# Low parts of weights moved from ScalarE and a DMA to VectorE, and a part of the last norm moved forward

## The chip, the cores and the metric

The kernel runs on one core of a Trainium2 chip. What counts is the time of one execution on the device in microseconds; the smaller, the better. The executions of the kernel before took 827.84, 830.14 and 832.91 us, a median of 830.14.

## What is computed

One encoder block on 512 tokens with 1024 channels, in float32. Cut to what matters here:

```python
h = rms_norm(x, norm1_pre)
q, k, v, z, xbc, dt_raw, gates = split_cols(h @ w_in, IN_SPLITS)
attn_out = gqa_attention(rope(norm(q)), rope(norm(k)), v) @ w_attn_proj
ssd_out = ssd_branch(z, xbc, dt_raw, ...) @ w_ssd_proj
g_attn, g_ssd = split(sigmoid(gates), 2)
x = x + rms_norm((g_attn * attn_out + g_ssd * ssd_out) @ w_out, norm1_post)
gate, up = split(rms_norm(x, norm2_pre) @ w_gate_up, 2)
x = x + rms_norm((silu(gate) * up) @ w_down, norm2_post)
```

## The kernel before

**Products in three matmuls.** Each float32 operand is split into a high part, rounded to float32r, and a low part, the difference to the original. `mm3` (L177) makes a product of two such pairs: low by high (L178), high by low (L179), high by high (L180).

**The stream of weights.** `weights()` (L103) lists the weights in the order in which they are used, each with the way in which its low part is made. `presplit()` (L136) takes the next raw weight, which SP has loaded (three buffers), and lets ScalarE write the high part (L144). For "v" VectorE and for "g" GpSimd subtracts it from the raw weight (L149). For "d" ScalarE writes the negated high part (L146: the negative of the rounded value, as its output is float32r) and a DMA started by GpSimd adds the weight to it from memory (L147). High and low parts have four buffers each, so a new weight's parts wait until TensorE has used the fourth before.

**The order of the work.** The setup norms x, transposes h and makes q. Then `kvproj` (L397) multiplies by w_kv in three chunks of the eight blocks of 128 channels (0 to 2, 3 to 5, 6 and 7): for each block k four token tiles with three matmuls each. VectorE makes h at L294 and the low part of its transposed form hT at L184 for the same product. Twelve weights w_xbc follow, then attention. `weave` sets matmuls of z (`zproj`, two column halves n with four weights each) and of the first two gates between the steps of attention (scores L635 and L636, maxima L638 and exponentials L641 of the softmax, its transposes L653), then the other fourteen gates between those of the SSD. Attention needs VectorE for the maxima, the division and copies. A scheduler orders the instructions of VectorE, ScalarE and GpSimd; each engine runs its own queue in order.

**The end.** `down` (L1153) makes the last product of the FFN with seven products of quarter matrices in place of eight, in this order of PSUM targets: u, v, a, x, u, a, y. Each runs in four groups; for a group ScalarE and VectorE split weights (L1195, L1196) and activations (L1201, L1202), and GpSimd starts a DMA (L1225) that adds a second block of the weight to the first. `add` (L1245) sums the results in tiles c[t, n], where t is the token tile and n the column half. `begin(t)` loads the residual x2, takes the square sum of one half on ScalarE (L155) and multiplies that half by the gain (L1257); `finish(t)` does so for the other half (L1264), forms the reciprocal root and writes the sum with the residual out (L1270). For tiles 0 and 1 `between` calls them after blocks 4 to 7 of the last product y; for tiles 2 and 3 `begin` is called behind the fifth product and `finish` when y is done.

Of the kernel before, what the change touches and what calls it, by code (L numbers as in the profile page):

```python
# [14 lines left out]
ALU = mybir.AluOpType  # L15
# [45 lines left out]
class Block:  # L61
# [41 lines left out]
    def weights(self):  # L103

        a = self.a
        for k0, kn in ((0, 3), (3, 3), (6, 2)):
            yield a["w_kv"][:, k0 : k0 + kn, :], kn * 288, "v" if k0 == 0 else "d"
        for j in range(12):
            yield a["w_xbc"][j], 1024, "g" if j < 3 else "d"
        for n in range(2):  # L110
            for i in range(4):
                yield a["w_z"][n, i], 1024, "gd"[n]
        for j in range(2 * KD):
            yield a["w_g"][j], 1024, "d"
        for j in range(KD):
            yield a["w_ap"][j], 512, "g"
        for j in range(KD):
            yield a["w_sp"][j], 1024, "g"
        for j in range(KD):
            yield a["w_o"][j], 1024, "gggggvvv"[j]  # L120
# [1032 lines left out]
    def down(self, pool):  # L1153


        V, A, G, T = self.V, self.A, self.G, self.T
# [5 lines left out]
        r1 = [new("r1", [256], PAIRS) for _ in range(PAIRS)]  # L1162
# [3 lines left out]
        def blk(g, k, n):  # L1166

            j = n0 + k * PAIRS + 2 * g
            return wd[j : j + 2, :, n * 512 : n * 512 + 512].rearrange("k p c -> p k c")
# [3 lines left out]
        for k in range(1, n0):  # L1173
# [5 lines left out]
            if k == 1:  # L1179
                gain = [new("gn", [512], 2) for _ in range(2)]  # L1180
# [7 lines left out]
        c = {(t, 1): cs.pop() for t in (2, 3, 0, 1)}  # L1188
# [22 lines left out]
        a11, a12 = (lambda k: act[n0 + k][:, lo]), (lambda k: act[n0 + PAIRS + k][:, lo])  # L1211
# [4 lines left out]
        def product(dst, b, a, start, after=None, sums=None, by_token=None, then=None):  # L1216

            kept = []

            def prep(g):  # L1220
                w = wsplit(b(g))
                for i in range(2):
                    kept.append((asplit(a(2 * g + i)), [y[:, i * 512 : i * 512 + 512] for y in w]))
                if after:
                    G.dma_start(chain[g], after(g), accum_op=ALU.add)  # L1225

            def work(g):
                for k in (2 * g, 2 * g + 1):
                    x, wi = kept[k]
                    for t in range(1 if by_token else 2):  # L1230
                        mm3(dst[t], [y[:, t * P : t * P + P] for y in x], wi, start and k == 0)
                    if sums:
                        sums(k)
                if g == NG2 - 1:
                    if by_token:
                        by_token()
                        for x, wi in kept:
                            mm3(dst[1], [y[:, P : 2 * P] for y in x], wi)
                    if then:
                        then()  # L1240

            stages.extend((lambda g=g: prep(g), lambda g=g: work(g)) for g in range(NG2))

        def add(t, n, p, op=ALU.add):
            V.tensor_tensor(c[t, n], c[t, n], p, op)  # L1245

        half = {}

        def begin(t):

            x = [new("x2", [512], 4) if t < 2 else self.slot("a", [512], name="x2") for _ in range(2)]
            for i in range(2):
                self.load(x[i], self.x2_d[t][:, i * 512 : i * 512 + 512])
            ss = self.tiny(2, "ss")
            self.square_sum(ss[:, 0:1], c[t, 1], self.rstd[:, t : t + 1])
            V.tensor_scalar(ss[:, 0:1], ss[:, 0:1], 1.0 / D, EPS, ALU.mult, ALU.add)
            V.tensor_tensor(c[t, 1], c[t, 1], gain[1], ALU.mult)  # L1257
            half[t] = x, ss

        def finish(t):  # L1260
            x, ss = half[t]
            r2 = self.rstd[:, t : t + 1]
            self.square_sum(ss[:, 1:2], c[t, 0], r2)
            V.tensor_tensor(c[t, 0], c[t, 0], gain[0], ALU.mult)  # L1264
            v = self.tiny(1, "rv")
            V.tensor_scalar(v, ss[:, 1:2], 1.0 / D, ss[:, 0:1], ALU.mult, ALU.add)
            r = self.rsqrt(v, 1, True)
            V.tensor_tensor(r, r, r2, ALU.mult)
            for i in (1, 0):
                V.scalar_tensor_tensor(c[t, i], c[t, i], r, x[i], ALU.mult, ALU.add)  # L1270
                self.load(self.out[t * P : t * P + P, i * 512 : i * 512 + 512], c[t, i])

        u = [self.ps("sa") for _ in range(2)]
        a = [self.ps("mm") for _ in range(2)]
        x = [self.ps("sb") for _ in range(2)]
        v, y = [bank[t, 0] for t in (0, 1)], [bank[t, 0] for t in (2, 3)]
# [12 lines left out]
        def second(p):  # L1289
            for t in range(2):  # L1290
                add(2 + t, 1, p[t], ALU.subtract)

        def sums6():
            for t in range(2):
                c[2 + t, 0] = cs.pop()
                A.copy(c[2 + t, 0], u[t])
                add(2 + t, 1, u[t], ALU.subtract)
                add(t, 1, u[t], ALU.subtract)
                add(2 + t, 0, x[t])
                begin(2 + t)  # L1300

        def sums3():
            for t in range(2):
# [1 line left out]

        def last(t):
            add(t, 0, y[t - 2])
            finish(t)

        between = {4: lambda: begin(0), 5: lambda: begin(1), 6: lambda: finish(0), 7: lambda: finish(1)}  # L1310
        product(u, lambda g: chain[g], a11, True, lambda g: blk(g, 0, 1),
                lambda k: V.tensor_tensor(r1[k], a22(k), a21(k), ALU.subtract), then=third_weights)
        product(v, lambda g: raw(g, 1, 0), a12, False, None, lambda k: V.tensor_tensor(a21(k), a11(k), a21(k), ALU.subtract),
                then=sums2)
        product(a, lambda g: chain[g], lambda k: r1[k], True, lambda g: blk(g, 1, 1),
                lambda k: V.scalar_tensor_tensor(r1[k], r1[k], -1.0, a11(k), ALU.mult, ALU.subtract), then=lambda: second(a))
        product(x, lambda g: p3[g], a21, True, None,
                lambda k: V.scalar_tensor_tensor(a12(k), r1[k], -1.0, a12(k), ALU.mult, ALU.subtract), then=lambda: second(x))
        product(u, lambda g: chain[g], lambda k: r1[k], False, lambda g: blk(g, 1, 0), then=sums6)
        product(a, lambda g: raw(g, 1, 1), a12, False, then=sums3)  # L1320
        product(y, lambda g: chain[g], a22, False, None, lambda k: between.get(k, int)(), lambda: last(2))
        stages[0][0]()
        for i, (_, work) in enumerate(stages):
            if i + 1 < len(stages):
                stages[i + 1][0]()
            work()
        last(3)

    @staticmethod
# [121 lines left out]
```

## Time and profile before

| what | value |
|---|---|
| median of the three executions | 830.14 us |
| the profiled execution, its own time | 830.12 us |
| its span in the profile | 828.2 us |
| TensorE busy | 804.9 us, 97% |
| VectorE busy | 578.4 us, 70% |
| ScalarE busy | 465.8 us, 56% |
| GpSimd busy | 200.0 us, 24% |

The profile shows one execution. Busy shares are means over stages with different limits; what a stage waits for is read from its own stretch of the trace.

### The profile page before, as it was taken

How to read it: one execution, taken by the hardware profiler on the slowest of the kernel's cores; microseconds unless marked ns; L12 is line 12 of the kernel's file. 1: busy time of each engine (PE TensorE's matmuls, PEld its weight loads, DVE VectorE, ACT ScalarE, POOL GpSimd, SP SyncE). 2: the span in 40 equal slices, each digit the busy share in tenths (PEclk: the TensorE clock that was granted, in tenths of full speed). 3: DMA queues.
4: the chain of work that ended last, by engine and by line, in shares of the span. 5: the costliest groups of instructions: out<-in, count | busy, mean ns of one | idle time of the engine just before them, and what ended most of it. 6: DMA issues, size and time to landing. Idle time of an engine off the chain costs nothing.

```text
span 828.2 us, 12209 instructions
## 1 busy us (share of the span) xinstructions
PE 804.9 (97%) x4522; PEld 676.8 (82%) x4522; DVE 578.4 (70%) x999; ACT 465.8 (56%) x841; POOL 200.0 (24%) x162
## 2 busy tenths in 40 slices
PE   8899999999899999999999999999999999999994
PEld 7688887666676777777888798999999999888883
DVE  3959785656335456685783799788888878837988
ACT  7767875745844442166333656555555555536673
POOL 3443430100132244539451002000000100041200
PEclk9999999999999999999999999999999999999998
DMA  9757830620875665137335453667766664899642
GB/s 314 218 134 159 200 93 27 140 64 1 216 176 130 158 150 124 52 114 252 116 129 185 164 153 91 188 193 188 193 177 185 182 178 140 286 288 245 104 93 102
DMA packets 49658, 130.52 MB, mean 158 GB/s; under 512 B 5568, under 2 KB 5952, under 8 KB 49600
## 3 DMA queue, kind: packets, MB, share of 16 engines
q1 hardware_dynamic: 38048, 95.46, 33.7%
q0 software_dynamic: 11552, 34.30, 24.0%
q8 instruction: 35, 0.57, 0.3%
q14 instruction: 23, 0.19, 0.1%
HBM read 121.35 MB, written 8.39 MB: 157 GB/s over the span
## 4 chain that ended last, share of the span: by engine, by line
PE 83%; DVE 5%; DMA 4%; ACT 3%; issue 2%; POOL 1%; SPq 1%; DVEq 0%; ACTq 0%; POOLq 0%
PE sa L972 10%; PE mm L178 8%; PE mm L179 8%; PE mm L180 8%; PE sc L972 7%; PE sb L1125 4%; PE sa L1125 4%; PE mm L972 3%; PE sb L972 3%; PE mm L1125 3%; PE sc L178 3%; PE sc L180 3%; PE sc L179 3%; PE sc L677 2%; PE sa L179 2%
## 5 line engine op out<-in xcount | busy, mean ns | idle before, releaser
L144 ACT CAST whi<-raw 128x1024 fp32r<-128x1024 f32 (+3 forms) x69 | 68.0, 992 | 20.6 <-PE sc L180 9.8
L178 PE MATMUL mm<-hT,wlo 128*128 128x512 f32 x176 | 73.8, 419 | 2.1 <-DMA wlo<-in_w_g 2.1
L149 POOL TENSOR_TENSOR wlo<-raw,whi 128x1024 fp32r<-128x1024 f32 (+1 forms) x28 | 58.2, 2081 | 65.5 <-ACT whi L144 63.9
L180 PE MATMUL mm<-hT,whi 128*128 128x512 f32 x176 | 69.7, 396 | 0.0
L179 PE MATMUL mm<-hT,whi 128*128 128x512 f32 x176 | 69.3, 394 | 0.0
L1023 POOL DMA_DIRECT2D raw<-in_w_gu x19 | 16.4, 861 | 211.5 <-ACT x L1114 54.8
L1028 ACT CAST whi<-raw 128x512 fp32r<-128x512 f32 (+1 forms) x57 | 41.6, 762 | 33.9 <-DMA raw<-in_w_gu 12.9
L1029 DVE TENSOR_TENSOR wlo<-raw,whi 128x512 fp32r<-128x512 f32 (+1 forms) x57 | 47.8, 866 | 16.3 <-ACT whi L1028 16.3
L972 PE MATMUL sa<-R,whi 128*128 128x256 f32 x304 | 56.4, 283 | 0.0
L972 PEld LDWEIGHTS sa<-R,whi 128*128 128x128 f32 x304 | 47.5, 192 | 0.0
L146 ACT ACTIVATE wlo<-raw 128x1024 fp32r<-128x1024 f32 (+2 forms) x31 | 32.3, 1043 | 26.4 <-PE mm L178 24.4
L972 PE MATMUL sa<-R,wlo 128*128 128x256 f32 x152 | 43.1, 283 | 0.0
L178 PEld LDWEIGHTS mm<-hT,wlo 128*128 128x128 f32 x176 | 33.3, 189 | 11.8 <-issue 3.2
L147 POOL DMA_DIRECT2D wlo<-in_w_g x16 | 13.8, 863 | 112.6 <-ACT wlo L146 66.7
L179 PEld LDWEIGHTS mm<-hT,whi 128*128 128x128 f32 x176 | 33.3, 189 | 8.7 <-issue 2.4
L180 PEld LDWEIGHTS mm<-hT,whi 128*128 128x128 f32 x176 | 33.3, 189 | 7.6 <-issue 0.5
L638 DVE TENSOR_REDUCE nmax<-sa 128x1 f32<-128x512 f32 x32 | 21.6, 686 | 19.9 <-PE sa L636 19.7
L972 PE MATMUL sa<-h2T,b 128*128 128x256 f32 x228 | 30.5, 283 | 0.0
L641 ACT ACTIVATE pr<-sa,nmax 128x512 f32<-128x512 f32 x32 | 22.0, 688 | 14.6 <-DVE rc L643 7.4
L972 PEld LDWEIGHTS sa<-R,wlo 128*128 128x128 f32 x152 | 29.2, 192 | 0.0
L155 ACT ACTIVATE junk<-z 128x512 bf16<-128x512 f32 x8 | 5.0, 628 | 42.6 <-DVE z L785 42.5
L972 PEld LDWEIGHTS sa<-h2T,b 128*128 128x128 f32 x228 | 28.7, 192 | 0.0
(475 smaller groups left out, 2552.8 us busy)
## 6 DMA issues: line engine op xcount, KB each, us to landing
raw<-in_w_gu SPq DMA_DIRECT2D x44, 512.0 KB, 4.7
raw<-in_w_gu POOLq DMA_DIRECT2D x19, 512.0 KB, 5.4
raw<-in_w_g SPq DMA_DIRECT2D x16, 512.0 KB, 6.0
wlo<-in_w_g POOLq DMA_DIRECT2D x16, 512.0 KB, 6.8
raw<-in_w_dn SPq DMA_DIRECT2D x14, 512.0 KB, 7.2
raw<-in_w_xbc SPq DMA_DIRECT2D x12, 512.0 KB, 4.9
ch<-in_w_dn POOLq DMA_DIRECT2D x12, 512.0 KB, 7.2
b<-in_w_gu SPq DMA_DIRECT2D x19, 256.0 KB, 5.8
```

The source lines that it names most:

```text
L144: self.A.copy(h[:, :n], raw[:, :n])
L146: self.A.mul(l[:, :n], raw[:, :n], -1.0)
L149: e.tensor_tensor(l[:, :n], raw[:, :n], h[:, :n].bitcast(F32), ALU.subtract)
L178: self.T.matmul(o, ll, rh, start=first, stop=False)
L179: self.T.matmul(o, lh, rl, start=False, stop=False)
L180: self.last_mm = self.T.matmul(o, lh, rh, start=False, stop=last)
L638: V.tensor_reduce(nmax, ps, AX.X, ALU.max, negate=True)
L641: self.last_exp = A.activation(pr, ps, AF.Exp, bias=nmax, accum_out=sm)
L972: self.T.matmul(dst, x, y[:, k], start=start and k == 0 and i == 0, stop=k == 3 and i == 2, skip_group_check=True)
L1028: A.copy(dst[0], src)
L1029: lo.tensor_tensor(dst[1], src, dst[0].bitcast(F32), ALU.subtract)
L1125: self.T.matmul(o, x, y, start=start and i == 0, stop=i == 2, skip_group_check=True)
```

## The change

Four entries of the stream of weights get another way: the second kv chunk, the second column half of z (four weights) and the first two gates have their low parts subtracted by VectorE instead of being made by ScalarE and an accumulating DMA. In the end stage `begin` and `finish` take the column half as an argument. For token tiles 0 and 1 the first column half, whose sum is complete after the fourth product, is begun there, in `third`; `finish` does the second half behind blocks 6 and 7 of y, and nothing stands behind blocks 4 and 5. The four multiplications by the gain in `begin` and two of the four in `finish` go from VectorE to GpSimd.

```diff
@@ weights @@
-            yield a["w_kv"][:, k0 : k0 + kn, :], kn * 288, "v" if k0 == 0 else "d"
+            yield a["w_kv"][:, k0 : k0 + kn, :], kn * 288, "d" if k0 == 6 else "v"
...
-                yield a["w_z"][n, i], 1024, "gd"[n]
+                yield a["w_z"][n, i], 1024, "gv"[n]
         for j in range(2 * KD):
-            yield a["w_g"][j], 1024, "d"
+            yield a["w_g"][j], 1024, "v" if j < 2 else "d"
@@ down @@
-        def begin(t):
+        def begin(t, n):
...
-            self.square_sum(ss[:, 0:1], c[t, 1], self.rstd[:, t : t + 1])
+            self.square_sum(ss[:, 0:1], c[t, n], self.rstd[:, t : t + 1])
             V.tensor_scalar(ss[:, 0:1], ss[:, 0:1], 1.0 / D, EPS, ALU.mult, ALU.add)
-            V.tensor_tensor(c[t, 1], c[t, 1], gain[1], ALU.mult)
+            G.tensor_tensor(c[t, n], c[t, n], gain[n], ALU.mult)
...
-        def finish(t):
+        def finish(t, n):
...
-            self.square_sum(ss[:, 1:2], c[t, 0], r2)
-            V.tensor_tensor(c[t, 0], c[t, 0], gain[0], ALU.mult)
+            self.square_sum(ss[:, 1:2], c[t, n], r2)
+            (G if t < 2 else V).tensor_tensor(c[t, n], c[t, n], gain[n], ALU.mult)
...
-            for i in (1, 0):
+            for i in (1 - n, n):
...
+        def third():
+            second(x)
+            for t in range(2):
+                begin(t, 0)
...
-                begin(2 + t)
+                begin(2 + t, 1)
...
-            finish(t)
-
-        between = {4: lambda: begin(0), 5: lambda: begin(1), 6: lambda: finish(0), 7: lambda: finish(1)}
+            finish(t, 0)
+
+        between = {6: lambda: finish(0, 1), 7: lambda: finish(1, 1)}
...
-                lambda k: V.scalar_tensor_tensor(a12(k), r1[k], -1.0, a12(k), ALU.mult, ALU.subtract), then=lambda: second(x))
+                lambda k: V.scalar_tensor_tensor(a12(k), r1[k], -1.0, a12(k), ALU.mult, ALU.subtract), then=third)
```

The order of the instructions moves in three places. The first is VectorE's queue in the kv product (wlo is a weight's low part, whi its high part; h and hT as above; the numbers only tell tiles apart). Before:

```order
L149 TENSOR_TENSOR wlo_356<-raw_135,whi_355 128x864
L184 TENSOR_TENSOR hT_343<-h_351,hT_341 128x512
L184 TENSOR_TENSOR hT_343<-h_359,hT_341 128x512
L294 SCALAR_TENSOR_TENSOR h_368<-xT_110,gcol_99,rbs_349 128x512
L294 SCALAR_TENSOR_TENSOR h_372<-xT_115,gcol_99,rbs_349 128x512
```

and now:

```order
L149 TENSOR_TENSOR wlo_356<-raw_135,whi_355 128x864
L184 TENSOR_TENSOR hT_343<-h_351,hT_341 128x512
L184 TENSOR_TENSOR hT_343<-h_359,hT_341 128x512
L149 TENSOR_TENSOR wlo_364<-raw_137,whi_363 128x864
L294 SCALAR_TENSOR_TENSOR h_367<-xT_110,gcol_99,rbs_349 128x512
L294 SCALAR_TENSOR_TENSOR h_371<-xT_115,gcol_99,rbs_349 128x512
```

The low part of the second chunk stands behind the second low part of hT, ahead of the third block's h and of all that follows.

The second is VectorE's queue in attention, where z is woven in (pt are transposed probabilities, aTl the low part of an attention result, nmax the maxima of the softmax, wst and stl belong to the decays). Before:

```order
L655 COPY pt_1582<-sb_1577 128x512
L506 TENSOR_TENSOR wst_1558<-wst_1558,dt_1353 128x128
L655 COPY pt_1596<-sb_1591 128x512
L184 TENSOR_TENSOR aTl_1628<-sc_1618,aTh_1627 128x512
L638 TENSOR_REDUCE nmax_1648<-sa_1645 128x1
L638 TENSOR_REDUCE nmax_1659<-sa_1656 128x1
```

and now:

```order
L655 COPY pt_1581<-sb_1576 128x512
L506 TENSOR_TENSOR wst_1557<-wst_1557,dt_1352 128x128
L149 TENSOR_TENSOR wlo_1691<-raw_1688,whi_1690 128x1024
L655 COPY pt_1595<-sb_1590 128x512
L149 TENSOR_TENSOR wlo_1697<-raw_1694,whi_1696 128x1024
L149 TENSOR_TENSOR wlo_1703<-raw_1700,whi_1702 128x1024
L184 TENSOR_TENSOR aTl_1627<-sc_1617,aTh_1626 128x512
L638 TENSOR_REDUCE nmax_1647<-sa_1644 128x1
L638 TENSOR_REDUCE nmax_1658<-sa_1655 128x1
L149 TENSOR_TENSOR wlo_1709<-raw_1706,whi_1708 128x1024
```

Three of the four low parts of z stand ahead of the low part of the attention result, one behind the next two maxima. The two gates' low parts stand together, between the low part of the next attention result and the next maximum:

```order
L184 TENSOR_TENSOR aTl_2072<-sc_2062,aTh_2071 128x512
L149 TENSOR_TENSOR wlo_2177<-raw_2174,whi_2176 128x1024
L149 TENSOR_TENSOR wlo_2183<-raw_2180,whi_2182 128x1024
L638 TENSOR_REDUCE nmax_2105<-sa_2102 128x1
```

Before, that result was followed by the maxima at once.

The third is GpSimd's queue in the last products (ch are weight tiles of the chain, c the sums, gn the gains). It held only DMAs before; now:

```order
L1225 DMA ch_7374<-in_w_dn 128x2x512
L1257 TENSOR_TENSOR c_7401<-c_7401,gn_7406 128x512
L1225 DMA ch_7375<-in_w_dn 128x2x512
L1257 TENSOR_TENSOR c_7400<-c_7400,gn_7406 128x512
L1225 DMA ch_7372<-in_w_dn 128x2x512
L1225 DMA ch_7373<-in_w_dn 128x2x512
L1225 DMA ch_7374<-in_w_dn 128x2x512
L1225 DMA ch_7375<-in_w_dn 128x2x512
L1257 TENSOR_TENSOR c_7405<-c_7405,gn_7407 128x512
L1257 TENSOR_TENSOR c_7404<-c_7404,gn_7407 128x512
L1264 TENSOR_TENSOR c_7403<-c_7403,gn_7407 128x512
L1264 TENSOR_TENSOR c_7402<-c_7402,gn_7407 128x512
```

The multiplications for tiles 0 and 1 stand on either side of the last chain DMA of the third product's set; the four others stand behind all DMAs.

## Rows read from the trace of the kernel before

**Rows 1.** The page, part 1: busy time, share of the span, instructions of TensorE.
```profile
PE 804.9 (97%) x4522; PEld 676.8 (82%) x4522; DVE 578.4 (70%) x999; ACT 465.8 (56%) x841; POOL 200.0 (24%) x162
```

**Rows 2.** Waits of TensorE in 150:180 and 200:222: total us, times, longest us.
```profile
PE mm L179 <- DMA wlo<-in_w_z: 1.8, 2, 1.3
...
PE mm L178 <- DMA wlo<-in_w_g: 2.1, 1, 2.1
```

**Rows 3.** TensorE's timeline: start, us, instruction, [idle before <- its end].
```profile
38.69 0.37 PE L179 MATMUL sb<-wlo,hT 128*128 128x288 f32 x1 [3.29 <-DMA wlo<-in_w_kv]
...
171.41 0.50 PE L179 MATMUL mm<-wlo,hT 128*128 128x512 f32 x1 [0.55 <-DMA wlo<-in_w_z]
...
213.09 0.62 PE L178 MATMUL mm<-hT,wlo 128*128 128x512 f32 x1 [2.08 <-DMA wlo<-in_w_g]
```

**Rows 4.** Stretches: length; busy us of PE, PEld, DVE, ACT, POOL; PEclk; DMA.
```profile
30.30:35.10 4.80, 4.80 (x37) 4.76 (x37) 4.80 (x7) 2.88 (x5) 2.94 (x3) 1.00 0.94 273
...
39.24:42.65 3.41, 3.41 (x16) 3.41 (x15) 1.09 (x2) 3.41 (x6) 0.31 (x1) 0.50 0.51 198
...
155.60:159.50 3.90, 3.90 (x17) 1.42 (x14) 0.02 (x1) 3.06 (x5) 1.70 (x2) 1.00 0.88 233
...
161.00:175.50 14.50, 12.67 (x71) 9.91 (x70) 10.48 (x25) 9.34 (x24) 0.85 (x1) 1.00 0.70 173
...
204.90:209.70 4.80, 4.80 (x22) 3.96 (x22) 0.00 (x0) 4.77 (x6) 1.42 (x2) 1.00 0.35 45
...
213.32:216.73 3.41, 3.41 (x9) 2.65 (x9) 0.76 (x2) 1.08 (x2) 0.00 (x0) 0.50 1.06 269
...
799.00:817.70 18.70, 18.38 (x80) 14.34 (x78) 18.39 (x42) 12.21 (x25) 0.00 (x0) 1.00 0.01 5
```

**Rows 5.** DMA issues in 18:62 and 150:172: count, KB each, us to landing.
```profile
wlo<-in_w_kv POOLq DMA_DIRECT2D x1, 432.0 KB, 8.7
...
wlo<-in_w_z POOLq DMA_DIRECT2D x4, 512.0 KB, 8.5
```

**Rows 6.** VectorE's timeline, 28 to 40 us.
```profile
27.65 1.05 DVE L149 TENSOR_TENSOR wlo<-raw,whi 128x864 fp32r<-128x864 f32 x1
...
33.62 4.21 DVE L294 SCALAR_TENSOR_TENSOR h<-xT,gcol,rbs 128x512 f32<-128x512 f32 x3
37.76 1.88 DVE L184 TENSOR_TENSOR hT<-h,hT 128x512 fp32r<-128x512 f32 x3
```

**Rows 7.** VectorE's groups by line, 700 to 829: busy us, mean ns.
```profile
L149 DVE TENSOR_TENSOR wlo<-raw,whi 128x1024 fp32r<-128x1024 f32 x6 | 7.2, 1224 | 1.3 <-ACT whi L144 1.3
...
L1257 DVE TENSOR_TENSOR c<-c,gn 128x512 f32<-128x512 f32 x4 | 2.7, 692 | 0.0
```

**Rows 8.** GpSimd's timeline, 28 to 40 us.
```profile
33.58 2.38 POOL L149 TENSOR_TENSOR wlo<-raw,whi 128x1024 fp32r<-128x1024 f32 x1 [1.82 <-ACT whi L144]
```

**Rows 9.** ScalarE's timeline, 155 to 166 and 200 to 216 us.
```profile
161.56 1.05 ACT L144 CAST whi<-raw 128x1024 fp32r<-128x1024 f32 x1
...
204.93 1.06 ACT L146 ACTIVATE wlo<-raw 128x1024 fp32r<-128x1024 f32 x1 [0.79 <-PE mm L179]
```

**Rows 10.** GpSimd's and VectorE's timelines, 480 to 520 and 494 to 504 us.
```profile
497.83 2.12 POOL L939 TENSOR_TENSOR R<-R,R 128x512 fp32r<-128x512 f32 x1 [0.71 <-ACT R L938]
...
498.74 1.77 DVE L934 SCALAR_TENSOR_TENSOR af<-R,af 128x512 f32<-128x512 f32 x1
```

**Rows 11.** GpSimd's timeline, 735 to 829 us.
```profile
768.79 1.20 POOL L1225 DMA_DIRECT2D ch<-in_w_dn  x1 [1.81 <-DVE wlo L1196]
```

**Rows 12.** VectorE's timeline, 760 to 829 us.
```profile
769.75 1.22 DVE L1196 TENSOR_TENSOR wlo<-p,whi 128x1024 fp32r<-128x1024 f32 x1
```

**Rows 13.** The chain that ended last: start, us, what.
```profile
773.39 10.88 PE sb L1125 x48
...
810.93 0.60 DVE c L1257
...
812.92 0.60 DVE c L1264
```

## The prediction

> **What bounds the kernel now.** I read the page first, then what TensorE waits for, then its timeline, then the engines that would take the moved work. TensorE is busy for 97% of the span [rows 1], so a change pays only by removing its idle stretches, by keeping its clock up, or by shortening what follows its last matmul. The list of waits and the timeline show what to look at: 3.29 us for the low part of the second kv chunk, 1.8 us in two pieces for low parts of z, 2.1 us for that of the first gate, each time for a DMA that GpSimd started [rows 2, 3]. These are the very weights that the change hands to VectorE.
>
> The reader should see two costs in each wait. One is the hole itself: TensorE stands still from 35.40 to 38.69 and from 211.01 to 213.09 [rows 3]. The other stands behind it: after the 3.29 us hole, 16 matmuls take 3.41 us with a granted clock of 0.50 (the 1.2 GHz level), where 37 of that kind took 4.80 us at 1.00 (2.4 GHz) before; after the 2.08 us hole nine more run in 3.41 us at 0.50 [rows 3, 4]. The two holes in z, of 1.3 and 0.55 us, lie in a stretch of full clock, 161.0 to 175.5 [rows 2 to 4].
>
> Why are the low parts late? For such a weight ScalarE writes the negated copy, GpSimd starts the DMA that adds the weight, and from issue to landing that DMA takes 8.7 us for a kv chunk and 8.5 for z [rows 5]. A subtraction of 128x1024 on VectorE takes 1.22 us, one of 128x864 takes 1.05 [rows 6, 7].
>
> **The kv chunk.** Removed: the 3.29 us hole and the slow stretch behind it. That stretch has 16 matmuls in 3.41 us; at full clock they take 4.80 / 37 = 0.130 each, 2.08 in all, so 1.3 is lost [rows 4]. Together 4.6.
> Added: one 128x864 subtraction of 1.05 us, a tenth of it beside its neighbour, which the order puts behind the second hT low part and ahead of three L294. What is late next is that queue, since the low parts of hT come from it: between 33.62 and 37.76 it is in three L294 that take 4.21 us, where the three L184 behind them, as large, take 1.88: GpSimd's L149 begins at 33.58, lasts 2.38 and holds the first of them [rows 6, 8]. The low part of k = 5, the first of the three L184 from 37.76 on, is now ready at 37.76 + 0.68 = 38.44 and would be ready at about 39.4. TensorE stood from 35.40, behind the first matmul of k = 3 (0.30 long, so from 35.10); a k is 12 matmuls, 12 x 0.130 = 1.56 us, so without the hole it wants k = 5 at 35.10 + 2 x 1.56 = 38.2, and the first matmul of each group (L178) is the one that reads hT's low part. So a new wait of 1.2 us stands there, of the size (1.3) that left the clock at full in z. Net -4.6 + 1.2 = **-3.4**. Ends: -4.6 if GpSimd's subtraction falls where it holds nothing and the wait is gone, -2.35 if the hold grows by the 1.05 us that VectorE was moved. I take -3.4, since the hold in the row is decided by 0.04 us and I have no row that moves it.
> The third chunk keeps its DMA. ScalarE's and GpSimd's steps for the second chunk are ahead of its own and fall away, so it starts no later than now, and its 288 KB, beside the second chunk's 432, should not take longer than that one's 8.7 us, which ended the hole at 38.69 [rows 3, 5], so it is there by about 39.5; it is wanted at 35.10 + 3 x 1.56 + 1.2 = 41.0: covered.
>
> **Half of z.** Four subtractions of 1.22 us replace four DMAs. VectorE is idle for 3.9 us just ahead of 159.56 [rows 4], where the order puts three of the four; the fourth stands behind the next two maxima. It is the one that TensorE waits for at 171.41; ScalarE makes its copy from 161.56 to 162.61 even with the negation ahead of it [rows 9], so VectorE has it by about 164.5. With both holes gone TensorE wants it at 171.41 - 0.55 - 1.3 = 169.6. The two holes go: 1.3 + 0.55, **-1.85** [rows 2, 3]. Ends: 0 if the softmax chain is pushed instead, and -2.2 if the restart behind each hole costs a tenth or two as well.
>
> **Two gates.** VectorE has nothing at all to do from 204.9 to 209.7 [rows 4], and both subtractions stand there in its queue. ScalarE no longer negates at 204.93 [rows 9], so its copy, as long as the negation within a tenth, takes that place, is done at 206.0, and the low part is ready at 207.3. TensorE wants it at 211.0 (213.09 less 2.08). Removed: 2.08 us, and the half clock: nine matmuls in 3.41 us from 213.32 on, where 22 took 4.80 at full clock, 3.41 - 9 x 0.218 = 1.45, and 0.2 more for the one at 213.09, 1.65 in all [rows 3, 4]: **-3.7**. The second gate's weight has no wait now, so its move brings nothing. Ends: 0 and -3.7. Seven negations of about 1.06 us [rows 9] leave ScalarE and seven accumulating DMAs GpSimd's queue; nothing waits for either engine there beyond the waits already counted. SP's loads of the raw weights stay.
>
> **The tail.** Six multiplications of 128x512 leave VectorE; each cost it 0.60 from issue to issue (0.69 in duration) [rows 7], 3.6 us in all, from a stretch of the last product in which it is busy 18.39 of 18.70 us [rows 4]. But GpSimd's multiplication reads SBUF, and so do VectorE's two-input operations: where GpSimd's L939 ran for 2.12 us, VectorE's L934 of that size took 1.77 us, not 0.69, so 1.08 of hold [rows 10]. Two holds, from the first column halves of tiles 0 and 1, fall at about 767 to 771, since GpSimd's queue now has these multiplications on either side of the chain DMA that starts at 768.79 [rows 11]. VectorE is full there, but its parts are early: the low part at 769.75 is finished at 770.97 for a product that starts at 773.39 [rows 12, 13], 2.4 us of margin against 2.2 us of hold. I cost them at nothing; if that cover is gone, 2.2 us. Of the other four I take three as held, since two of them run beside additions that read PSUM: 3 x 1.08 - 3.6 = **-0.4**. Ends: +2.9 (six holds that each cost 1.08 - 0.60 = 0.48), and -2.4, the four multiplications of 0.60 that stand in the chain from 810.93 to 813.52 [rows 13], with no hold at all.
> By the Trainium skill (SBUF — State Buffer, "Who interferes with whom") whoever of VectorE and GpSimd issues first holds the shared port pair for a whole instruction, when VectorE's instruction has two SBUF inputs. The L934 row agrees (1.77 against 0.69). By that rule alone all six would be held wherever VectorE has two-input work, +2.9 in place of -0.4; this is a rival below.
>
> **Sum.** -3.4 - 1.85 - 3.7 - 0.4 = -9.35, against the profiled execution of 830.12 us, within 0.02 of the median of the three runs (830.14): 820.8 us.
>
> **Rivals.**
> 1. *The six multiplications are all held and the margin at 773 is used up.* For it: VectorE is nearly full in the whole last stage. Against it: that margin [rows 12, 13]. 830.12 - 3.4 - 1.85 - 3.7 + 2.9 = 824.1.
> 2. *The kv gain is eaten, or never comes.* The chunk that stays with the DMA arrives after 41.0, or the xbc weights behind it, whose pace is set by their loads and not by kv, make TensorE wait as much longer. 820.8 + 3.4 = 824.2. Against: the chunk is the smaller one, and TensorE waits for no xbc weight now.
> 3. *Softmax becomes the bound.* Without holes in z and gate, TensorE waits for rows of probabilities that VectorE now makes later; -1.85 and -3.7 are lost: 820.8 + 5.55 = 826.3. For it: the maxima of softmax stand right behind the subtractions in VectorE's queue. Against: both idle stretches are longer than the work put into them (3 x 1.22 = 3.7 in 3.9, 2 x 1.22 = 2.4 in 4.8) [rows 4, 7].
> 4. *Slower.* VectorE takes its queue in order. If a subtraction heads the queue while its ScalarE copy waits for TensorE to give back a weight buffer, the maxima and copies of softmax behind it wait too, and TensorE for them. Each of six such places would cost copy, subtraction and hand-over, 1.06 + 1.22 and an estimated 0.25, 2.5, in all 15 [rows 7, 9]: 820.8 + 15 = 835.8. It decides from 9.35 / 6 = 1.6 us of delay at each place on. Against: the idle stretches again.
>
> **How the numbers follow.** Chances: forecast 0.58, first rival 0.16, second 0.11, third 0.10, slower 0.05. A measurement of this kernel tells about 0.5%, 4.15 us, from no change: faster is below 826.0. Forecast and the first two rivals are faster, 0.85; the third lies at the edge, within, 0.10; slower 0.05. The range begins at 817.2, the sum of the good ends kv -4.6, z -2.2, gates -3.7, tail -2.4 (-12.9), and reaches to 825.5 over the first two rivals with some of their spread; the third and the fourth, 0.15, are left out.
>
> **What would show it.** In the waits of TensorE the three DMA entries are gone, and one of about 1.2 us for VectorE's hT low part (L184) stands near 38 to 39. The granted clock is 1.00 from 35 to 45 and from 209 to 217. The last kv chunk shows no wait. VectorE's L149 at 128x1024 has six more instructions of 1.22 us, three of them in the former idle stretch. GpSimd shows six multiplications of 1.3 to 2.1 us, and some neighbours on VectorE 1.1 us too long. I am wrong if TensorE's waits for softmax rows (L635, L653) grow by as much as the DMA waits shrink, if the time from the seventh product's start to the end grows by over 1 us, or if a wait for an xbc or a kv weight appears.

## The result, and the profile after the change

Four executions of the changed kernel took 820.67 to 821.49 us, a median of 821.06, against 831.39 for the kernel before beside them (827.84 to 832.91): a ratio of 0.9884, with a 95% interval from 0.9857 to 0.9910. That is 10.3 us by the medians. The profiled execution took 821.49 us, 8.6 less than that of before (830.12); its span is 819.7 us.

What TensorE waits for now, over the whole span (total us, times, longest us):

```profile
PE sa L268 <- DVE ones L264: 1.1, 1, 1.1
PE sb L178 <- DVE hT L184: 0.9, 1, 0.9
...
PE sc L1125 <- DVE wlo L1196: 0.6, 1, 0.6
```

All DMA entries of [rows 2, 3] are gone. In the place of the 3.29 us in kv stands a wait of 0.9 for hT's low part, as expected; the 0.6 in the last product is new.

Stretches of the changed kernel (columns as in [rows 4]):

```profile
35.00:39.00 4.00, 4.00 (x31) 3.82 (x29) 4.00 (x4) 0.92 (x2) 2.38 (x1) 1.00 0.77 210
39.99:45.00 5.01, 5.01 (x37) 5.01 (x38) 2.51 (x5) 5.01 (x9) 1.16 (x1) 1.00 0.18 67
156.00:166.00 10.00, 10.00 (x53) 8.15 (x52) 9.05 (x20) 6.95 (x16) 0.00 (x0) 1.00 0.37 127
202.00:217.00 15.00, 14.91 (x80) 10.98 (x80) 9.15 (x18) 14.55 (x27) 1.72 (x2) 1.00 0.80 213
784.00:808.80 24.80, 24.03 (x104) 18.86 (x102) 21.53 (x42) 14.01 (x28) 6.38 (x4) 1.00 0.21 63
```

The granted clock is 1.00 where it was 0.50 in [rows 4], and TensorE has no hole left in z or at the gate. Only the last line, from just ahead of the sixth of the seven products to TensorE's last matmul, is clearly not full (24.03 of 24.80 us).

VectorE's timeline in the kv product, with the new subtraction at 30.34:

```profile
30.34 1.05 DVE L149 TENSOR_TENSOR wlo<-raw,whi 128x864 fp32r<-128x864 f32 x1
31.31 2.07 DVE L294 SCALAR_TENSOR_TENSOR h<-xT,gcol,rbs 128x512 f32<-128x512 f32 x3
33.30 1.89 DVE L184 TENSOR_TENSOR hT<-h,hT 128x512 fp32r<-128x512 f32 x3
35.11 4.22 DVE L294 SCALAR_TENSOR_TENSOR h<-xT,gcol,rbs 128x512 f32<-128x512 f32 x3
39.26 1.88 DVE L184 TENSOR_TENSOR hT<-h,hT 128x512 fp32r<-128x512 f32 x3
```

The three L294 are held again, 4.22 us where the three before take 2.07, as in [rows 6]. Further on, the same view has the last three low parts of z and the two of the gates:

```profile
152.40 2.35 DVE L149 TENSOR_TENSOR wlo<-raw,whi 128x1024 fp32r<-128x1024 f32 x2
...
158.78 1.22 DVE L149 TENSOR_TENSOR wlo<-raw,whi 128x1024 fp32r<-128x1024 f32 x1
...
200.65 1.23 DVE L149 TENSOR_TENSOR wlo<-raw,whi 128x1024 fp32r<-128x1024 f32 x1 [1.38 <-ACT whi L144]
202.04 1.23 DVE L149 TENSOR_TENSOR wlo<-raw,whi 128x1024 fp32r<-128x1024 f32 x1 [0.16 <-ACT whi L144]
```

They take 1.2 us each. VectorE waits 1.38 us for ScalarE's copy once, and nothing was due there: behind the two it still waits 0.86 us for TensorE's next scores (L636).

The end stage went the other way. GpSimd's timeline there:

```profile
755.85 1.19 POOL L1225 DMA_DIRECT2D ch<-in_w_dn  x1 [1.61 <-DVE wlo L1196]
757.41 8.26 POOL L1257 TENSOR_TENSOR c<-c,gn 128x512 f32<-128x512 f32 x1 [0.38 <-ACT junk L155]
765.62 1.19 POOL L1225 DMA_DIRECT2D ch<-in_w_dn  x1
766.39 1.75 POOL L1257 TENSOR_TENSOR c<-c,gn 128x512 f32<-128x512 f32 x1
...
790.66 1.29 POOL L1257 TENSOR_TENSOR c<-c,gn 128x512 f32<-128x512 f32 x1 [11.18 <-ACT junk L155]
...
800.87 3.75 POOL L1264 TENSOR_TENSOR c<-c,gn 128x512 f32<-128x512 f32 x2 [6.68 <-ACT junk L155]
```

One multiplication that takes 1.29 us by itself took 8.26, and the chain DMA behind it started 34.6 us after the first of the seven products (731.05), where it started 28.2 after it before (768.79 - 740.59). The half that it multiplies is complete with the second product (the last addition to it is in `sums2`), not with the fourth, so that the scheduler could put it as early as the third. VectorE at the same time and later:

```profile
764.43 0.21 DVE L1256 TENSOR_SCALAR ss<-ss 128x1 f32<-128x1 f32 x2
764.55 2.21 DVE L1196 TENSOR_TENSOR wlo<-p,whi 128x1024 fp32r<-128x1024 f32 x1
...
790.54 0.15 DVE L1256 TENSOR_SCALAR ss<-ss 128x1 f32<-128x1 f32 x1 [2.24 <-ACT junk L155]
...
793.02 2.25 DVE L1196 TENSOR_TENSOR wlo<-ch,whi 128x1024 fp32r<-128x1024 f32 x1
```

and ScalarE, where the last raw weight comes in, first before and then now:

```profile
796.82 1.05 ACT L1195 CAST whi<-raw 128x1024 fp32r<-128x1024 f32 x1 [1.04 <-DMA raw<-in_w_dn]
...
788.74 1.05 ACT L1195 CAST whi<-raw 128x1024 fp32r<-128x1024 f32 x1 [2.51 <-DMA raw<-in_w_dn]
789.70 0.71 ACT L155 ACTIVATE junk<-c,rstd 128x512 bf16<-128x512 f32 x1
```

VectorE is held twice (2.21 and 2.25 us for an L1196 of 1.22), and between the two it stands idle for 2.24 us, since ScalarE waits 2.51 us for a raw weight. Where did the 8.6 us of the two profiles come from? TensorE's first matmul of the seven products starts at 731.05 instead of 740.59, 9.5 us earlier; from there to the end of the span it is 88.65 us instead of 87.61, 1.0 more. So the weights gave more than forecast (8.95), and the end stage cost where -0.4 was forecast.

### The profile page after: what moved, and what is told of

The parts are those of the page before. It is cut to its first block, busy times and chain, and to the rows that moved or that the text cites. A ratio compares the mean times of both kernels' runs of the same rounds, so it can differ in the third digit from the quotient of the medians.

```text
span 819.7 us, 12211 instructions
## 1 busy us (share of the span) xinstructions
PE 801.7 (98%) x4522; PEld 674.1 (82%) x4522; DVE 584.1 (71%) x1000; ACT 458.9 (56%) x834; POOL 209.6 (26%) x161
## 4 chain that ended last, share of the span: by engine, by line
PE 84%; DVE 6%; ACT 3%; DMA 3%; issue 2%; POOL 2%; SPq 0%; DVEq 0%; ACTq 0%; POOLq 0%
PE sa L972 10%; PE mm L178 8%; PE mm L179 8%; PE mm L180 8%; PE sc L972 7%; PE sa L1125 4%; PE sb L1125 4%; PE mm L972 3%; PE sb L972 3%; PE mm L1125 3%; PE sc L178 3%; PE sc L179 3%; PE sc L180 3%; PE sc L677 2%; PE sb L653 2%
## 5 line engine op out<-in xcount | busy, mean ns | idle before, releaser
L1029 DVE TENSOR_TENSOR wlo<-raw,whi 128x512 fp32r<-128x512 f32 (+1 forms) x57 | 49.1, 889 | 17.0 <-ACT whi L1028 16.7
L147 POOL DMA_DIRECT2D wlo<-in_w_g x14 | 12.1, 862 | 145.1 <-PE mm L179 81.1
L146 ACT ACTIVATE wlo<-raw 128x1024 fp32r<-128x1024 f32 (+1 forms) x24 | 25.1, 1047 | 24.4 <-PE mm L178 24.3
L149 DVE TENSOR_TENSOR wlo<-raw,whi 128x1024 fp32r<-128x1024 f32 (+1 forms) x17 | 20.2, 1201 | 16.6 <-ACT whi L144 10.1
L1196 DVE TENSOR_TENSOR wlo<-ch,whi 128x1024 fp32r<-128x1024 f32 x16 | 20.4, 1281 | 13.2 <-ACT whi L1195 13.1
```

The source lines that it names most:

```text
L146: self.A.mul(l[:, :n], raw[:, :n], -1.0)
L149: e.tensor_tensor(l[:, :n], raw[:, :n], h[:, :n].bitcast(F32), ALU.subtract)
L1029: lo.tensor_tensor(dst[1], src, dst[0].bitcast(F32), ALU.subtract)
L1196: V.tensor_tensor(l, src, h.bitcast(F32), ALU.subtract)
```

## The experiments

Every kernel has executions of the kernel before beside it; these spread over 825.4 to 832.9 us, those with all the new low parts, four executions each, over under 2 us each. The executions of before beside the experiments come in three sets, with medians of 829.33, 829.45 and 829.37 us; those beside the change have 831.39. Differences of under 2 us are therefore read from the kernels' own times and from the lengths of stages in their profiles. Stage lengths of the end, from the timelines (first of the seven products, TensorE's end, span), with the start of the fifth product's first chain DMA and of the copy of the last raw weight, both counted from the first of the seven products:

| kernel | chain DMA | raw weight | to TensorE's end | from there to the span's end | sum |
|---|---|---|---|---|---|
| before | 40.1 | 56.2 | 77.14 | 10.47 | 87.61 |
| weights_only | 39.4 | 55.1 | 76.32 | 10.18 | 86.50 |
| kv_only | 39.6 | 55.5 | 76.39 | 10.47 | 86.86 |
| w_xbc0v | 39.9 | 55.7 | 76.63 | 10.42 | 87.05 |
| old_order_g | 39.4 | 55.1 | 76.32 | 10.74 | 87.06 |
| the change | 41.0 | 57.7 | 77.75 | 10.90 | 88.65 |
| tail_only | 41.0 | 57.3 | 77.38 | 11.27 | 88.65 |
| all_on_v | 40.7 | 57.1 | 78.05 | 9.38 | 87.43 |
| early_on_v | 40.7 | 56.9 | 77.07 | 10.76 | 87.83 |
| one_input | 42.9 | 60.0 | 80.13 | 10.91 | 91.04 |
| mid_begin_v | 39.3 | 55.4 | 76.32 | 9.38 | 85.70 |

**1. The weights without the end stage.** The change with `down` as before, that is:

```diff
+            yield a["w_kv"][:, k0 : k0 + kn, :], kn * 288, "d" if k0 == 6 else "v"
+                yield a["w_z"][n, i], 1024, "gv"[n]
+            yield a["w_g"][j], 1024, "v" if j < 2 else "d"
```

> Seven low parts by VectorE, the end stage as before. The profile of the change shows TensorE's work up to the first of the seven last products 9.5 us earlier, and everything from there to the end 1.0 us longer. If the moved multiplications are what costs that 1.0 us, this kernel is the faster of the two: about 820.0 us, 87.4 to 87.5 us from the start of the first of the seven products to the end of the span, as before, and no wait of TensorE for a weight's low part in the last product. Rival: the 1.0 us comes with any order in which these products start earlier, or is chance of one execution; then it takes about 821.1 us, like the change, with 88.4 us behind that start.

Measured: 818.97 us (818.66 to 820.24), 829.33 for before beside it, ratio 0.9896 (0.9862 to 0.9930). It is 2.1 us faster than the change, and their executions do not overlap. The end stage takes 86.50 us. So the moved norm costs, and more than the 1.0 us that the two first profiles show: the old stage itself took 86.5 to 87.6 us in the profiles with it. The ratios alone would not say so (0.9884 for the change), as the executions of before beside the change took longer than those of the other sets; the lengths of the stage and experiment 2 say it.

**2. The end stage alone.** Only `down` changed.

> The end stage of the change, the weights as before. If the end stage costs 1.0 us by itself: 831 us where before has 830.1 to 831.4, 88.4 us from the start of the first of the seven products to the end; GpSimd's first multiplication takes about 8 us again, as long as VectorE runs instruction after instruction with both inputs in SBUF. By the prediction's term (-0.4) 830 us and 87.0 us; by a GpSimd multiplication that is only held by one instruction of VectorE it takes at most 1.3 + 1.2 = 2.5 us.

Measured: 831.61 us (828.04 to 834.36), ratio 1.0036 (1.0013 to 1.0058): slower by 2.3 us of medians, 3.0 by the ratio. The stage takes 88.65 us, and GpSimd's first multiplication 8.25 us. The prediction's -0.4 is refuted, and so is the picture of a GpSimd instruction held by one of VectorE's.

**3. One kind of weight at a time.** Each with one of the three lines above.

> Only the second half of z goes to VectorE. By the prediction -1.85 us, by the shift of TensorE's starts in the change's profile -2.15: about 828.1 us against 830.1, no wait of TensorE for a low part of z. The wait for the first gate (2.1 us) with the half clock behind it stays. Rival: with the z holes gone the wait for the gate's DMA grows by as much, since that DMA's start hangs on ScalarE and not on TensorE; then nothing is gained, 830 us, and the gate's wait is 4 us.

> Only the two gates go to VectorE. By the prediction -3.7 us, by the shift of starts in the change's profile -4.0: about 826.3 us against 830.1, with a granted clock of 1.00 all the way from 205 to 222 us. Rival: part of those 4 us came from z's being earlier as well; then under 3 us, and a wait of TensorE for a softmax row or for another gate shows in 205 to 260 us.

> Only the second kv chunk goes to VectorE. By the prediction -3.4 us; by the length of the kv stage in the profiles (16.2 us from its first matmul to its hundredth-odd before, 12.4 with the change, 11.5 without its end stage) -3.8 to -4.6: about 825.5 us against 829.3, no half clock from 38 to 44 us. Rival: the twelve xbc weights eat it, and TensorE waits for one of them or for a weight of z by as much: 829 us.

Measured: z 825.40 us (823.87 to 830.38), ratio 0.9965 (0.9944 to 0.9987); gates 826.64 (823.74 to 828.58), ratio 0.9978 (0.9962 to 0.9994), both beside 829.33; kv 825.29 (824.25 to 827.09) beside 829.45, ratio 0.9951 (0.9935 to 0.9968). By medians -3.9, -2.7 and -4.2, in sum -10.8; together they gave -10.4 (experiment 1). As far as the scatter lets one tell, none eats what another gives: the rivals that had the gate's wait grow, or the xbc weights eat kv's gain, fall.

z gave more than its two holes. With z alone the gate's hole stays, and TensorE's timeline and stretches show it:

```profile
210.85 0.50 PE L178 MATMUL mm<-hT,wlo 128*128 128x512 f32 x1 [2.09 <-DMA wlo<-in_w_g]
```

```profile
210.70:216.00 5.30, 5.15 (x27) 4.22 (x27) 3.42 (x10) 3.72 (x7) 0.00 (x0) 1.00 1.07 281
```

The hole is as long as in [rows 3], yet the clock behind it is 1.00, not 0.50. In this profile TensorE's starts are 0.15 us later than before ahead of the z holes, 2.25 earlier behind them and 3.83 earlier behind the gate. What else sets the clock behind such a hole was not tried; but part of the gates' forecast belongs, in this one profile, to whatever comes ahead of them. In kv_only, where z's waits stand, the gate's hole is 2.33 and the clock from 209.9 to 214.0 is 0.58.

**4. The second gate left with the DMA.** Experiment 1 with `"v" if j < 1 else "d"` for the gates.

> Seven low parts less that of the second gate, which stays with ScalarE and the DMA; old end stage. By the prediction the second gate's move brings nothing: 819.0 us as with it (818.97), and no wait of TensorE for a gate's low part. Rival: with the first gate 9 us earlier the second is wanted before its DMA has landed; then a wait for that DMA at 218 to 225 us, and 820 us or more.

Measured: 819.39 us (818.91 to 820.38), with no wait for a gate's low part. Its move brings nothing that can be told.

**5. The hold in kv.** Experiment 1, and

```diff
-            yield a["w_xbc"][j], 1024, "g" if j < 3 else "d"
+            yield a["w_xbc"][j], 1024, "vgg"[j] if j < 3 else "d"
```

> The seven low parts on VectorE with the old end stage, and the first xbc weight's low part on VectorE too instead of GpSimd. GpSimd's subtraction no longer falls on VectorE's h of the last three blocks, so that those take 2.1 us and not 4.2, and TensorE's wait for hT's low part in the kv product (0.93 in the change, 0.2 in the run without its end stage) goes. By the prediction's term that wait is set by the hold: 0.2 to 0.9 us less than with the old assignment, 818.1 to 818.8 us against 818.97. Rival: VectorE's added 1.2 us comes too late for the first xbc product; then a wait of TensorE for that weight's low part at 43 to 45 us and no gain.

Measured: 818.27 us (817.42 to 819.22), ratio 0.9867 (0.9848 to 0.9886). VectorE's timeline:

```profile
34.85 2.07 DVE L294 SCALAR_TENSOR_TENSOR h<-xT,gcol,rbs 128x512 f32<-128x512 f32 x3
36.83 1.88 DVE L184 TENSOR_TENSOR hT<-h,hT 128x512 fp32r<-128x512 f32 x3
38.64 1.21 DVE L149 TENSOR_TENSOR wlo<-raw,whi 128x1024 fp32r<-128x1024 f32 x1
```

The three L294 take 2.07 us, not 4.22, and no wait for hT is left. So GpSimd's subtraction was what held them. The gain of 0.7 by medians lies within the forecast, but the executions overlap with those of experiment 1.

**6. All multiplications back on VectorE, or the two early ones.** Both are the change with the engine of one or two lines edited:

```diff
-            G.tensor_tensor(c[t, n], c[t, n], gain[n], ALU.mult)
+            V.tensor_tensor(c[t, n], c[t, n], gain[n], ALU.mult)
...
-            (G if t < 2 else V).tensor_tensor(c[t, n], c[t, n], gain[n], ALU.mult)
+            V.tensor_tensor(c[t, n], c[t, n], gain[n], ALU.mult)
```

and, for the second kernel, `(V if t < 2 else G)` in `begin` only.

> The change with all eight multiplications by the gain on VectorE, so that only the earlier norm of two half tiles is left of the end stage's edit. If what costs there is GpSimd standing between VectorE and the chain's DMAs, this kernel loses the 8 us multiplication, the raw weight of the last product lands in time, and the end stage takes no more than with the old order: about 87.0 us from the start of the first of the seven products (87.45 before, 88.5 in the change), 819.0 us in all, against 821.06 for the change and 818.97 with the old end stage. Rival: it is the earlier square sums and residual loads that cost; then it stays at 821.

> The change with only the two early multiplications (tiles 0 and 1 behind the fourth product) on VectorE, the four later ones left on GpSimd. If the 8.3 us multiplication in front of a chain DMA is the cause, the chain's DMA that stood behind it starts 6 us earlier, TensorE's wait for a low part in the last product (0.6 us) goes, and the end stage takes 87.0 to 87.5 us, 819 to 819.5 us in all. Rival: the four later multiplications cost by their holds and by standing late (3.75 us for two); then half of the loss or more stays, 820.3 us or over.

Measured: 820.16 us (819.84 to 820.36) and 820.85 (820.61 to 822.25). Both expectations fail by over 1 us; the second kernel meets its rival (820.3 or over), the first lies between expectation and rival. The 8 us multiplication is gone in both and the DMA behind it is on time again, at 27.5 us, yet the fifth product's chain DMAs still start at 40.7 us, the raw weight is still late (57.1 and 56.9 us), and TensorE still ends late (78.05 and 77.07). So GpSimd standing in the queue was not the main cause. What all kernels with the early norm share is 1 us or more of added time on VectorE ahead of the fifth product's low parts: 0.99 us of hold in the change (2.21 - 1.22), two multiplications of 0.60 in these. VectorE has no gap in the change from 754 to 780 us, so its own queue sets when these low parts are ready, and not a wait for ScalarE's earlier square sums. They release the chain DMAs, which start 1.3 to 1.5 us later than in experiment 1 and run beside the load of the last raw weight. That load is issued 48.8 us after the first of the seven products before and in experiment 1, and 48.9 to 49.1 in the change and these two kernels; from issue to landing it took 7.4 and 6.2 us there, and 8.0 to 8.5 here. That it is the chain DMAs beside it that make it longer is argued from their times; no run moved them alone. The residual loads, which the first rival names, are no cause: all are issued ahead of the first of the seven products, before (from 722.4 us on) as in the change (712.9) and with all multiplications on VectorE (713.0).

The four later multiplications have a price of their own. With them on GpSimd TensorE ends 1.0 us earlier (77.07 against 78.05), but from there to the end of the span it takes 1.4 us more (10.76 against 9.38).

**7. The early norm a little later.** All low parts as in experiment 5, all multiplications on VectorE, no `third`, but

```diff
+            self.last_wlo = V.tensor_tensor(l, src, h.bitcast(F32), ALU.subtract)
...
+        def soon(t):
+            with self.tc.issue_after(self.last_wlo.ins):
+                begin(t, 0)
+
+        early = {5: lambda: soon(0), 7: lambda: soon(1)}
...
+        product(u, lambda g: chain[g], lambda k: r1[k], False, lambda g: blk(g, 1, 0),
+                lambda k: early.get(k, int)(), then=sums6)
```

> All low parts as in the best run so far (818.27), all multiplications on VectorE, and the first column halves of tiles 0 and 1 begun behind the low parts of the fifth product's weights, whose chain DMAs VectorE's work had delayed when the halves were begun behind the fourth. If that delay is the whole cost of the early norm, the chain's DMAs start 39.4 to 40.1 us behind the start of the seven products as with the old order (40.7 to 41.0 in the three kernels with the early norm), TensorE ends 76.3 to 76.7 us behind it, and the shorter queue at the end still gives what it gave with all multiplications on VectorE, 9.4 us from TensorE's end to the end of the span instead of 10.4: 86.0 us in all and 817.3 us for the kernel. Rival: the two halves cost wherever they stand, since VectorE is full up to the end; then 818.3 or more.

Measured: 817.70 us (817.41 to 818.91), ratio 0.9866 (0.9846 to 0.9887). The stage takes 85.70 us, 76.32 + 9.38, as expected within 0.3. VectorE's timeline shows the halves behind the last low part that releases a chain DMA:

```profile
775.11 1.23 DVE L1196 TENSOR_TENSOR wlo<-ch,whi 128x1024 fp32r<-128x1024 f32 x1
776.25 0.15 DVE L1256 TENSOR_SCALAR ss<-ss 128x1 f32<-128x1 f32 x1
776.32 0.68 DVE L1257 TENSOR_TENSOR c<-c,gn 128x512 f32<-128x512 f32 x1
```

The chain DMAs are on time (39.3 us), and the load of the last raw weight takes 6.5 us. The norm forward is worth having, 1.0 us behind TensorE's end (9.38 against 10.42), once it does not stand ahead of the DMAs. This kernel is the best of the study: 3.4 us below the change by medians, with no overlap. From experiment 5 its executions cannot be told apart; only the stage length (85.70 against 87.05) does it.

**8. The multiplications on GpSimd in the old order.** Experiment 1, with six of the eight on GpSimd.

> Seven low parts on VectorE, the old order of the end stage, but the same number of multiplications on GpSimd as in the change (all four of the first kind and two of the second). By the prediction's term, three or four holds against 3.6 us of work taken from VectorE: -0.4 to +0.8 us against the run with the same low parts (818.97), so 818.6 to 819.8. If a GpSimd multiplication in the last product can stand still for as long as VectorE's two-input instructions follow each other, those of tiles 0 and 1 end late, 3 us or more each, and the end comes later: 820 us or over.

Measured: 820.04 us (819.45 to 820.91), 1.1 above experiment 1, at the rival's edge. TensorE ends after 76.32 us, as in experiment 1, so the holds cost it nothing; what is lost lies from TensorE's end on (10.74 us against 10.18), where GpSimd is late. Its timeline:

```profile
798.12 3.75 POOL L1257 TENSOR_TENSOR c<-c,gn 128x512 f32<-128x512 f32 x2 [6.68 <-ACT junk L155]
801.83 2.54 POOL L1264 TENSOR_TENSOR c<-c,gn 128x512 f32<-128x512 f32 x2
```

Of the 1.1 us these 0.6 are shown in the end stage; the kv stage of this profile was longer too (12.24 us against 11.51 for its first 84 matmuls), which the edit doesn't touch.

**9. What ends GpSimd's 8 us.** The change, and in `prep` of the fourth product

```diff
+                if dst is x:
+                    V.tensor_scalar(w[1][:, 0:1], w[1][:, 0:1].bitcast(F32), 1.0, None, ALU.mult)
```

> The change with four instructions of VectorE more, each on one column (128x1) of a low part in the fourth product, with one input in SBUF; the multiplication by 1.0 leaves the values as they are. In the change GpSimd's first multiplication takes 8.3 us and ends 1.1 us behind the first 128x1 instruction in VectorE's queue. If GpSimd is shut out by consecutive two-input instructions and let in at the first one with a single input, it now ends at the first of the added ones, about 3.5 us earlier, so lasts 4.5 to 5 us, and the chain DMA behind it starts 31 us behind the start of the seven products instead of 34.6. Rival: GpSimd's multiplication waits for something else that comes at that time (the square sum's step, a DMA); then it takes 8 us again.

Measured, one execution: 824.36 us. The timelines of GpSimd and VectorE (the two added lines make L1257 here L1259, and so on):

```profile
757.59 5.11 POOL L1259 TENSOR_TENSOR c<-c,gn 128x512 f32<-128x512 f32 x1 [0.37 <-ACT junk L155]
762.64 1.20 POOL L1227 DMA_DIRECT2D ch<-in_w_dn  x1
```

```profile
761.45 0.15 DVE L1223 TENSOR_SCALAR wlo<-wlo 128x1 fp32r<-128x1 f32 x1
761.51 1.46 DVE L1202 TENSOR_TENSOR as<-act,as 128x256 fp32r<-128x256 f32 x1
762.90 2.89 DVE L1325 SCALAR_TENSOR_TENSOR act<-r,act 128x256 f32<-128x256 f32 x2
```

The multiplication now ends 1.25 us behind the first added instruction and holds the one behind it (1.46 us instead of 0.42); it took 5.11 us, and the DMA starts 31.1 us behind the first of the seven products. So an instruction of VectorE with one input in SBUF let GpSimd in here; whether the single input does it or the shortness of the instruction (128x1) is not told apart. The kernel is slower by 3 us: VectorE is now held by both early multiplications, by 1.04 us and, with the second one, by 2.1 (two L1325 in 2.89 us instead of 0.76). The fifth product's chain DMAs start at 42.9 us, the load of the raw weight takes 8.9 us, and TensorE ends at 80.13: later DMAs again go with a later end.

## Why the prediction was right, and where it was not

The forecast was 820.8 us, measured were 821.06. The sum is right partly by luck: the low parts gave more than forecast (-10.4 by medians in experiment 1, forecast -8.95), and the tail cost where it was to give.

*kv, forecast -3.4, alone -4.2.* The steps hold: no hole, full clock, and in its place a wait for hT's low part behind the held L294. The wait was put at 1.2 us and measured 0.9 in the change and in kv_only, 0.2 to 0.9 in the other profiles with the same edit, none where the hold is gone (experiment 5). What sets it between 0.2 and 0.9 was not tried. The third chunk landed in time: its DMA, issued at 30.69 us, took 8.1, though the premise for it was not safe (in the kernel before it took 9.0 us, longer than the second chunk's 8.7).

*z, forecast -1.85, alone -3.9 by medians (-1.1 to -4.6 by the ratio's interval).* The holes went as said, and 2.4 us with them in TensorE's starts. The rest is, by the one profile of z_only, the clock behind the gate's hole, which I had booked whole to the gate.

*Gates, forecast -3.7, alone -2.7 by medians (-0.5 to -3.2 by the ratio's interval).* Hole and half clock are gone, as said. The second gate's move brings nothing, as said. Alone, z and gates gave -6.6 together by medians, where both terms make -5.55.

*The tail, forecast -0.4, measured +2.1 beside the new low parts (821.06 - 818.97) and +2.3 alone (831.61 - 829.33).* The step that failed is this one: "I cost them at nothing", for two holds with "2.4 us of margin against 2.2 us of hold". The margin was that of the product which starts next. But VectorE's low parts also release the chain DMAs of the fifth product; these slid by 0.9 us against the kernel before (1.5 against experiment 1), and the copy of the last raw weight by 1.5 (2.6). ScalarE then copied late, VectorE waited 2.24 us in its queue, and TensorE ended 0.6 later (1.4 against experiment 1). The price of a hold was wrong too: I had one instruction's length (1.08) for either side, and GpSimd's multiplication stood for 8.26. And taking work from VectorE gave nothing behind TensorE's end: 10.90 us against 10.18 in experiment 1. One of the prediction's own signs of being wrong is there: from the seventh product's start to the end it is 23.37 us instead of 22.33, 1.04 more, where "over 1 us" was the sign.

*The rivals.* Softmax did not become the bound: three of z's low parts ran in the idle stretch or just ahead of it, with 1.61 us of it left over, and the fourth behind the two maxima, with no new wait of TensorE. The slower rival's mechanism shows, at a harmless place: the gates' subtractions wait 1.38 and 0.16 us for their copies, below its limit of 1.6, and TensorE waits for nothing behind them. The first rival, that the multiplications eat 2.9 us, came nearest to what happened to the tail, by another path.

## What to carry to other kernels

An instruction that is moved ahead into a full queue must be weighed against everything that this queue releases, the DMAs too: here the next product had 2.4 us to spare, and a load two products on had none. A low part that an engine with an idle stretch can make in 1.2 us was better there than behind a DMA of 8 to 9 us. Work given from VectorE to GpSimd was priced here by the run of VectorE's instructions beside it, not by its own length.

## What was unexpected of the hardware

GpSimd's multiplication stood for 8.26 us beside fourteen instructions of VectorE that follow each other without a gap and have both inputs in SBUF, and got in at the first with a single input (764.43; 761.45 in experiment 9). The Trainium skill (SBUF — State Buffer, "Who interferes with whom") has whoever issues first hold the shared port pair for the whole instruction, with the other one blocked; the holds of one instruction (2.21 and 2.25 us instead of 1.22) agree with that, and the 8.26 us show besides that the blocked one may lose many times in a row. It isn't always so: in [rows 10], and at 35.1 us in the kv product, GpSimd got in between two such instructions. What decides there was not tried.

The granted clock behind a hole of 2.1 us in TensorE's work was 0.50 in the kernel before and 1.00 in z_only, with the same instructions on either side.

The kernel before scattered over 7 us in all its executions beside the others, each kernel with all the new low parts, in four executions, over less than 2; why was not tried. In the profiles with the kv chunk on a DMA the kv stage took 15.3 to 17.2 us for its first 84 matmuls (the holes are 2.7 to 3.7 us long); with VectorE it took 11.1 to 12.4.
